# One pool of eight PSUM banks for dense and small products, and the second GLA pair in the order k, q, v, k, q, g

## The chip, the core and the metric

One core of a Trainium2 chip runs the whole program. The metric is the device time of that core in microseconds (us), the median of several executions. TensorE (PE) multiplies, VectorE (DVE), ScalarE (ACT) and GpSimd (POOL) do the element work, and SyncE (SP) issues nearly all DMAs. A PSUM bank takes the output of a matrix product; there are eight of them, each as wide as a 128 x 512 float32 tile.

## The reference, cut to what matters

Two layers on one sequence of 512 tokens, model width 1024. Each layer normalizes x, projects it by one wide matrix `w_in`, and hands the columns to three mixers that work beside each other:

```python
h = rmsnorm(x, norm_mix_g[l])
proj = h @ w_in[l]
y_gla = gla_mixer(a_q, a_k, a_v, a_gk, a_g, ...)      # 4 heads, key 128, value 256
y_ssm = ssd_mixer(b_z, b_xbc, b_dt, ...)              # 4 groups of 8 heads
y_diff = diff_mixer(c_q, c_k, c_v, positions, ...)    # 8 heads, softmax pairs
mixed = (gates[:, :, 0] * (y_gla @ w_br_gla[l]) + gates[:, :, 1] * (y_ssm @ w_br_ssm[l])
         + gates[:, :, 2] * (y_diff @ w_br_diff[l]))
x = x + mixed @ w_out[l]
x = x + jnp.square(jax.nn.relu(rmsnorm(x, norm_mlp_g[l]) @ w_mlp_up[l])) @ w_mlp_down[l]
```

A GLA head needs its own key columns k, query columns q, value columns v and output gate columns g of `proj`; its state runs over chunks of the sequence and its scores carry a decay per key channel. The output is normalized once more at the end.

## The kernel before, in words

All large products are made in float32 precision from three products of rounded parts: a weight block is split into a high part `whi` (ACT) and a rest `wlo` (DVE, or POOL when that ends sooner), the activations lie split in `hl`, and PE adds hi x hi, hi x lo and lo x hi in one bank. Three such products are called a triple below.

The program is written out by a planner that runs in Python before compilation. Class `Flow` keeps a clock of its own (that of PE), a cost model of the engines (`Model`), a list of dense **items** and a list of small **tasks** (generators). `Flow.run` (L445) always serves a task whose wait is met before it takes up a dense step; the order in which PE, ACT, DVE and POOL get their instructions is the order of the planned times. On the chip an engine works through its list in that order and waits on semaphores.

Dense items are of three shapes. `item_a` (L871) makes one 128 x 512 output in one bank, from two half blocks of weights of four triples each; k, q, the SSD inputs and the branch gates are of this shape. `item_a2` (L897) makes two outputs in two banks, for the SSD branch product. `item_w` (L946) makes four 128 x 512 outputs, one per 128 tokens, in four banks that are all open through its eight half blocks of four triples; the value item v and the gate item g of a GLA pair and the q, k, v items (cq, ck, cv) of a differential pair are of this shape. Its first half block asks for the four banks one at a time:

```python
for t in range(NT):
    if i == 0:
        yield {"d": 1}
        it.banks.append(self.T("d"))
```

`refill` (L376) takes the first of the next 28 items whose buffers and conditions are met and loads its weights through SP (L513); two raw weight buffers exist, and four pairs `whi`, `wlo`, of which two are split ahead (`LEAD`).

PSUM is shared out by two tags (L670): `d` with four banks for dense outputs, `m` with four for small products (transposes, scores, states; `psm`, L688). A bank is taken when a product is planned and goes back when its last reader is done. `tag` (L300), `free_at` (L303), `take` (L306) and `next_time` (L338) keep those counts.

A layer's items are listed in `layer` (L1897): `gla_duo` for heads 0 and 1 with the dt item between v and g, four SSD groups (with eight gate items among them, and the branch product of each group after the next group's items), then `gla_duo` (L1340) for heads 2 and 3, the branch product of the last SSD group, two differential pairs, the other 16 gate items, `w_br_gla`, `w_br_diff`, `w_out` and the MLP. For the first pair the items come as v, dt, g and then k, q of both heads; for the second as k, q, k, q, v, g. The items of a pair's v hold four `z4` buffers until both heads have used them, g and each differential item hold two, and there are eight.

`gla_head` (L1394) lists k and q and starts the head's tasks: `gates` (L1415, two DMAs through SP, a small product of the low-rank gate at L1428, logarithms and a scan along the tokens), `keys`, `scores` (L1489: seven levels, each a subtraction on POOL at L1518, two exponentials on ACT, two products with k and q, and small products on PE) and `finish` per chunk. They wait for the events of k and q, and for free `tt` buffers (11 in all).

`step` (L1766) is one softmax step of a differential head; the second differential pair's result goes through `parted` (L1757) to `w_br_diff`, which waits for both pairs.

Of the kernel before, what the change touches and what calls it, by code (L numbers as in the profile page):

```python
# [19 lines left out]
PSUM = bass.MemoryType.PSUM  # L20
# [13 lines left out]
O_Q, O_K, O_V, O_GK, O_G = 0, 512, 1024, 2048, 2064  # L34
# [11 lines left out]
class Event:  # L46
    def __init__(self):
        self.t = None


class Buf:
    def __init__(self, flow, tag, tile_):
        self.flow, self.tag, self.ap, self.rel, self.users = flow, tag, tile_, None, 1
# [12 lines left out]
QN = 6  # L66
FETCH = 4.5
WAKE = 14
LEAD = 2
LAT = {"V": 0.13, "A": 0.1, "G": 0.05}  # L70

# [213 lines left out]
class Flow:  # L285


    def __init__(self, nc):
        self.nc = nc
        self.clock = 0.0  # L290
        self.model = Model(self, nc)
        self.cap, self.pool, self.live = {}, {}, {}
        self.tasks = []
        self.items = []
        self.queue = []
        self.cur = None
        self.hold = None
        self.booked, self.end = [], 0.0

    def tag(self, name, pool, cap):  # L300
        self.cap[name], self.pool[name], self.live[name] = cap, pool, []

    def free_at(self, tag, at):  # L303
        return self.cap[tag] - sum(1 for b in self.live[tag] if b.rel is None or b.rel > at)

    def take(self, tag, shape, dt=F32):  # L306
        live = self.live[tag]
        held = sum(1 for b in live if b.rel is None)
        assert held < self.cap[tag], tag
        b = Buf(self, tag, self.pool[tag].tile(shape, dt, name=tag, bufs=self.cap[tag]))  # L310
        if tag in ("d", "m"):
            self.model.banks.add(b.ap.tensor.name)
        if len(live) >= self.cap[tag]:
            old = min((x for x in live if x.rel is not None), key=lambda x: x.rel)
            self.model.base[b.ap.tensor.name] = old.rel
            live.remove(old)
        live.append(b)
        return b
# [19 lines left out]
    def next_time(self, w):  # L338
        if w is None:
            return self.clock  # L340
        if isinstance(w, (int, float)):
            return w
        if isinstance(w, Event):
            return w.t if w.t is not None else math.inf
        if isinstance(w, dict):
            r = self.clock
            for t, n in w.items():
                rel = sorted(math.inf if b.rel is None else b.rel for b in self.live[t]
                             if b.rel is None or b.rel > self.clock)
                over = len(rel) + n - self.cap[t]  # L350
                if over > 0:
                    r = max(r, rel[over - 1])
            return r
        return max([self.next_time(x) for x in w], default=self.clock)

# [39 lines left out]
    def stage(self):  # L395
# [4 lines left out]
        for j, (_, _, w) in enumerate(self.queue):  # L400
# [4 lines left out]
            if w.bufs is None:  # L405
                if j < LEAD + (self.cur is None) and self.spare("whi"):
                    w.split()
# [246 lines left out]
class Trunk:  # L654
    def __init__(self, tc, ctx, a, out):
        self.tc, self.a, self.out = tc, a, out
        self.ctx = ctx
        self.f = Flow(tc.nc)
        self.halves = [slice(0, S // 2), slice(S // 2, S)]
        self.nc = self.f.model  # L660
        self.const = self.pool("const", 1)
        self.dram = self.pool("dram", 1, space=DRAM)
        self.wp = self.pool("w", 2)
        mx = self.pool("mx", 1)
        self.mx = mx
        self.sm = Ring(self.nc, self.pool("sm", 4), 4)
        self.lp = Ring(self.nc, self.pool("lp", 1), 1)
        pd = self.pool("pd", 1, space=PSUM)
        pm = self.pool("pm", 1, space=PSUM)
        for name, p, cap in (("whi", self.wp, 4), ("wlo", self.wp, 4), ("wraw", self.wp, 2), ("res", mx, KT), ("hl", mx, 10), ("pj", mx, 10), ("z4", mx, 8), ("tw", mx, 3),  # L670
                             ("tt", mx, 11), ("g1", mx, 4), ("d", pd, 4), ("m", pm, 4)):
            self.f.tag(name, p, cap)

    def pool(self, name, bufs, **kw):
        return self.ctx.enter_context(self.tc.tile_pool(name=name, bufs=bufs, **kw))
# [664 lines left out]
    def gla_duo(self, l, duo, h, slot, evy, between=lambda: None, before=()):  # L1340
        nc, a, f = self.nc, self.a, self.f
        w = a["w_in"][l]
        V, G = nc.vector, nc.gpsimd
        first = duo == 0
        shared = {"evv": Event(), "evg": Event(), "r4": (lambda c: h.r4[:, c:c + 1]) if first else None}

        def vg_item(c0, gate):
            key = "g" if gate else "v"

            def fin(it, t, ps):  # L1350
                if first:
                    f.spawn(scaled(it, t, ps))
                else:
                    store(it, t, ps)

            def scaled(it, t, ps):
                yield h.evr4
                store(it, t, ps)

            def store(it, t, ps):  # L1360
                x = it.held[t // 2].ap[:, t % 2]
                if gate:
                    self.act(x, ps.ap, AF.Tanh, scale=h.r4h[:, t:t + 1] if first else 0.5)
                    V.scalar_tensor_tensor(x, x, 1.0, ps.ap, op0=ALU.add, op1=ALU.mult)
                    x2 = x.rearrange("p (h c) -> p h c", c=256)
                    G.tensor_tensor(x2, x2, self.gnr.unsqueeze(1).broadcast_to([P, 2, 256]), op=ALU.mult)
                elif first:
                    r = h.r4[:, t:t + 1]
                    self.act(x, ps.ap, AF.Copy, scale=r)
                    V.scalar_tensor_tensor(it.held[2 + t // 2].ap[:, t % 2], ps.ap, r, x.bitcast(F32),  # L1370
                                           op0=ALU.mult, op1=ALU.subtract)
                else:
                    self.split(x, it.held[2 + t // 2].ap[:, t % 2], ps.ap)
                ps.free()
                if t == NT - 1:
                    for b in it.held:
                        b.users = 2
                    shared[key] = it.held
                    shared["ev" + key].t = f.at(*[b.ap for b in it.held])
            self.item_w(w, c0, h.xg if first else h, fin, extra=[("z4", ([P, 2, S],))] * 2 if gate else  # L1380
                        [("z4", ([P, 2, S], F32R))] * 4, chain=first and not gate)

        def heads():
            for hd in (2 * duo, 2 * duo + 1):
                self.gla_head(l, hd, h, shared, slot, evy[hd], before)
        if not first:
            heads()
        vg_item(O_V + duo * 512, False)
        between()
        vg_item(O_G + duo * 512, True)  # L1390
        if first:
            heads()

    def gla_head(self, l, hd, h, shared, slot, evy, before):  # L1394
        nc, a, f = self.nc, self.a, self.f
# [656 lines left out]
    def load_x(self, ns):  # L2052
# [16 lines left out]
        wake = self.psm()  # L2069
        for i in range(WAKE):  # L2070
            f.tr(wake.ap[:, i % 4 * P:(i % 4 + 1) * P], self.ident, self.ident)
# [137 lines left out]
```

## Time and profile before

| what | value |
|---|---|
| median of 3 runs (lowest to highest) | 2758.38 us (2756.08 to 2759.82) |
| the profiled execution | 2758.74 us |
| its span, first to last instruction | 2756.9 us |
| granted TensorE clock, mean over the span | 0.994 |
| PE busy | 2712.4 us (98%) |
| DVE busy | 1785.3 us (65%) |
| ACT busy | 1311.7 us (48%) |
| POOL busy | 549.0 us (20%) |
| DMA, mean | 107 GB/s |

The page gives the busy time of each engine, the span in 40 slices, and the chain of work that ended last. Other views list who waited for whom, the instructions of a stretch in order of time with the idle time before each in square brackets and what released it, and the busy time of every engine in stretches that one names. A name such as `d<-whi,hl` gives the output tile and the two inputs, the moving operand first: `d<-whi,hl` and `d<-wlo,hl` are the products of an `item_w`, `d<-hl,whi` and `d<-hl,wlo` those of `item_a` and `item_a2`. The planner's helper records most instructions of DVE, ACT and POOL under L83, so tiles and not lines tell them apart. PEclk is the granted share of TensorE's full clock.

### The profile page before, as it was taken

How to read it: one execution, taken by the hardware profiler on the slowest of the kernel's cores; microseconds unless marked ns; L12 is line 12 of the kernel's file. 1: busy time of each engine (PE TensorE's matmuls, PEld its weight loads, DVE VectorE, ACT ScalarE, POOL GpSimd, SP SyncE). 2: the span in 40 equal slices, each digit the busy share in tenths (PEclk: the TensorE clock that was granted, in tenths of full speed). 3: DMA queues.
4: the chain of work that ended last, by engine and by line, in shares of the span. 5: the costliest groups of instructions: out<-in, count | busy, mean ns of one | idle time of the engine just before them, and what ended most of it. 6: DMA issues, size and time to landing. Idle time of an engine off the chain costs nothing.

```text
span 2756.9 us, 40684 instructions
## 1 busy us (share of the span) xinstructions
PE 2712.4 (98%) x14970; PEld 2227.5 (81%) x14970; DVE 1785.3 (65%) x3817; ACT 1311.7 (48%) x2670; POOL 549.0 (20%) x607
## 2 busy tenths in 40 slices
PE   9999999999999999999999999998999999999998
PEld 7788888768888888888877788877788888888887
DVE  7787787766767655444578777677847675644445
ACT  6666555543656333222356664555456652333222
POOL 2313242230221002101012322323222200011001
PEclk9999999999999999999999999999999999999999
DMA  5344434324234433333342443342332344333332
GB/s 163 95 107 128 113 108 134 87 81 126 70 96 122 126 118 97 93 100 97 95 132 74 123 130 103 104 137 76 108 89 84 88 129 146 107 100 98 93 100 85
DMA packets 448644, 293.92 MB, mean 107 GB/s; under 512 B 16614, under 2 KB 409436, under 8 KB 448444
## 3 DMA queue, kind: packets, MB, share of 16 engines
q1 hardware_dynamic: 447828, 290.26, 36.9%
q8 instruction: 118, 1.93, 0.3%
q10 hardware_dynamic: 616, 1.06, 0.1%
q14 instruction: 82, 0.67, 0.1%
HBM read 272.20 MB, written 19.07 MB: 106 GB/s over the span
## 4 chain that ended last, share of the span: by engine, by line
PE 74%; DVE 3%; ACT 1%; DMA 1%; issue 1%; SPq 0%; DVEq 0%; ACTq 0%
PE d L370 66%; PE m L370 6%; PE m L374 2%; DVE rs_t L83 1%; DVE wlo L83 0%; ACT tw L83 0%; DMA wraw<-in_w_in 0%; DVE tt L83 0%; DVE rs_y L83 0%; DVE pj L83 0%; DVE hl L83 0%; ACT whi L83 0%; ACT tt L83 0%; DMA tt<-in_gla_w_gk 0%; DVE g L83 0%
## 5 line engine op out<-in xcount | busy, mean ns | idle before, releaser
L370 PE MATMUL d<-hl,whi 128*128 128x512 f32 (+2 forms) x5696 | 1774.5, 393 | 3.3 <-DVE z L83 1.7
L370 PEld LDWEIGHTS d<-hl,whi 128*128 128x128 f32 (+1 forms) x5696 | 1046.5, 188 | 214.5 <-issue 3.1
L370 PE MATMUL d<-hl,wlo 128*128 128x512 f32 (+2 forms) x2848 | 1108.9, 389 | 6.2 <-DVE wlo L83 6.2
L83 ACT ACTIVATE whi<-wraw 128x512 fp32r<-128x512 f32 x868 | 542.5, 628 | 1044.2 <-PE d L370 956.1
L83 DVE TENSOR_TENSOR wlo<-wraw,whi 128x512 fp32r<-128x512 f32 (+1 forms) x817 | 594.3, 733 | 463.8 <-ACT whi L83 456.2
L370 PEld LDWEIGHTS d<-hl,wlo 128*128 128x128 f32 (+1 forms) x2848 | 533.9, 187 | 122.7 <-DVE wlo L83 9.6
L370 PE MATMUL d<-whi,hl 128*128 128x512 f32 x1280 | 408.7, 401 | 13.4 <-DVE z L83 12.3
L83 POOL TENSOR_TENSOR tt<-tt 128x512 f32<-128x512 f32 x128 | 160.8, 1266 | 942.4 <-ACT hl L83 779.7
L370 PEld LDWEIGHTS d<-whi,hl 128*128 128x128 f32 x1280 | 234.9, 190 | 60.4 <-issue 7.3
L370 PE MATMUL d<-wlo,hl 128*128 128x512 f32 x640 | 252.5, 395 | 3.2 <-DVE wlo L83 3.2
L370 PEld LDWEIGHTS d<-wlo,hl 128*128 128x128 f32 x640 | 121.4, 190 | 30.6 <-DVE wlo L83 4.1
L83 POOL TENSOR_TENSOR wlo<-wraw,whi 128x512 fp32r<-128x512 f32 x51 | 66.5, 1304 | 375.5 <-ACT whi L83 353.6
L83 DVE TENSOR_TENSOR res<-res,d 128x512 f32<-128x512 f32 (+1 forms) x130 | 86.9, 674 | 71.6 <-PE d L370 71.4
L83 DVE SCALAR_TENSOR_TENSOR pj<-d,cols,pj 128x511 f32<-128x511 f32 (+1 forms) x144 | 106.9, 745 | 17.9 <-ACT pj L83 16.0
L83 POOL TENSOR_TENSOR tw<-tw,tt 128x1024 f32<-128x1024 f32 x32 | 79.2, 2474 | 120.1 <-ACT tw L83 120.1
L83 DVE SCALAR_TENSOR_TENSOR tt<-d,tt 128x512 f32<-128x512 f32 x64 | 44.0, 690 | 80.0 <-PE d L370 77.4
L83 ACT ACTIVATE tt<-m 128x512 f32<-128x512 f32 (+5 forms) x132 | 59.0, 452 | 75.1 <-PE m L370 43.4
L83 ACT ACTIVATE tt<-tt 128x256 f32<-128x256 f32 (+3 forms) x190 | 87.6, 499 | 13.5 <-DVE tt L83 10.1
L83 ACT ACTIVATE tw<-tw,acn 128x128 f32<-128x128 f32 x256 | 83.2, 390 | 8.2 <-DMA tw<-acs 8.1
L83 ACT ACTIVATE pj<-m 64x256 fp32r<-64x256 f32 (+1 forms) x160 | 66.2, 420 | 34.9 <-PE m L374 16.4
L370 PEld LDWEIGHTS m<-z,tt 128*128 128x128 f32 x488 | 69.4, 190 | 12.0 <-DVE hl L83 2.5
L370 PE MATMUL m<-z,tt 128*128 128x128 f32 (+1 forms) x488 | 75.4, 284 | 3.4 <-DVE hl L83 2.0
(182 smaller groups left out, 2464.8 us busy)
## 6 DMA issues: line engine op xcount, KB each, us to landing
wraw<-in_w_in SPq DMA_DIRECT2D x224, 512.0 KB
wraw<-in_w_mlp_up SPq DMA_DIRECT2D x64, 512.0 KB
wraw<-in_w_mlp_down SPq DMA_DIRECT2D x64, 512.0 KB
tw<-acs SPq DMA_DIRECT2D x32, 512.0 KB
wraw<-in_w_br_ssm SPq DMA_DIRECT2D x32, 512.0 KB
gates<-tt SPq DMA_DIRECT2D x48, 256.0 KB
tt<-gates SPq DMA_DIRECT2D x48, 256.0 KB
wraw<-in_w_br_gla SPq DMA_DIRECT2D x16, 512.0 KB
```

The costliest lines, as they stand in the source:

```text
L83: fn = lambda a=args, k=kw: real(*a, **k)
L370: self.model.post(self.clock - c, lambda: self.nc.tensor.matmul(out, lhsT, rhs, start=start, stop=stop))
L374: self.model.post(self.clock - 0.109, lambda: self.nc.tensor.transpose(out, in_, ident))
```

## The change

The two tags keep their names, but their tiles now come from one tag `bank` of eight banks in one pool. `d` may hold up to six of them, `m` up to five, both together eight. A tag with a home has two limits, its own and the home's, and every count (free now, free at a time, when next) looks at both. The second pair's items are listed as k, q of head 2, v, k, q of head 3, g, and each head's tasks start with its k and q. The first pair stays as it was. No arithmetic changes, and no item, small product or DMA is added or removed.

```diff
--- before.py
+++ after.py
@@ -66,6 +66,7 @@
 QN = 6
 FETCH = 4.5
 WAKE = 14
+DBANKS, MBANKS = 6, 5
 LEAD = 2
 LAT = {"V": 0.13, "A": 0.1, "G": 0.05}
 
@@ -290,6 +291,7 @@
         self.clock = 0.0
         self.model = Model(self, nc)
         self.cap, self.pool, self.live = {}, {}, {}
+        self.home, self.limits = {}, {}
         self.tasks = []
         self.items = []
         self.queue = []
@@ -297,20 +299,25 @@
         self.hold = None
         self.booked, self.end = [], 0.0
 
-    def tag(self, name, pool, cap):
+    def tag(self, name, pool, cap, home=None):
+
         self.cap[name], self.pool[name], self.live[name] = cap, pool, []
+        self.home[name] = home or name
+        self.limits[name] = [name] + ([home] if home else [])
 
     def free_at(self, tag, at):
-        return self.cap[tag] - sum(1 for b in self.live[tag] if b.rel is None or b.rel > at)
+        return min(self.cap[t] - sum(1 for b in self.live[t] if b.rel is None or b.rel > at)
+                   for t in self.limits[tag])
 
     def take(self, tag, shape, dt=F32):
-        live = self.live[tag]
-        held = sum(1 for b in live if b.rel is None)
-        assert held < self.cap[tag], tag
-        b = Buf(self, tag, self.pool[tag].tile(shape, dt, name=tag, bufs=self.cap[tag]))
-        if tag in ("d", "m"):
+        home = self.home[tag]
+        assert all(self.spare(t) for t in self.limits[tag]), tag
+        b = Buf(self, tag, self.pool[tag].tile(shape, dt, name=home, bufs=self.cap[home]))
+        if home == "bank":
             self.model.banks.add(b.ap.tensor.name)
-        if len(live) >= self.cap[tag]:
+            self.live[tag] = [x for x in self.live[tag] if x.rel is None or x.rel > self.clock] + [b]
+        live = self.live[home]
+        if len(live) >= self.cap[home]:
             old = min((x for x in live if x.rel is not None), key=lambda x: x.rel)
             self.model.base[b.ap.tensor.name] = old.rel
             live.remove(old)
@@ -344,12 +351,13 @@
             return w.t if w.t is not None else math.inf
         if isinstance(w, dict):
             r = self.clock
-            for t, n in w.items():
-                rel = sorted(math.inf if b.rel is None else b.rel for b in self.live[t]
-                             if b.rel is None or b.rel > self.clock)
-                over = len(rel) + n - self.cap[t]
-                if over > 0:
-                    r = max(r, rel[over - 1])
+            for tag, n in w.items():
+                for t in self.limits[tag]:
+                    rel = sorted(math.inf if b.rel is None else b.rel for b in self.live[t]
+                                 if b.rel is None or b.rel > self.clock)
+                    over = len(rel) + n - self.cap[t]
+                    if over > 0:
+                        r = max(r, rel[over - 1])
             return r
         return max([self.next_time(x) for x in w], default=self.clock)
 
@@ -666,10 +674,11 @@
         self.sm = Ring(self.nc, self.pool("sm", 4), 4)
         self.lp = Ring(self.nc, self.pool("lp", 1), 1)
         pd = self.pool("pd", 1, space=PSUM)
-        pm = self.pool("pm", 1, space=PSUM)
         for name, p, cap in (("whi", self.wp, 4), ("wlo", self.wp, 4), ("wraw", self.wp, 2), ("res", mx, KT), ("hl", mx, 10), ("pj", mx, 10), ("z4", mx, 8), ("tw", mx, 3),
-                             ("tt", mx, 11), ("g1", mx, 4), ("d", pd, 4), ("m", pm, 4)):
+                             ("tt", mx, 11), ("g1", mx, 4), ("bank", pd, 8)):
             self.f.tag(name, p, cap)
+        for name, cap in (("d", DBANKS), ("m", MBANKS)):
+            self.f.tag(name, pd, cap, "bank")
 
     def pool(self, name, bufs, **kw):
         return self.ctx.enter_context(self.tc.tile_pool(name=name, bufs=bufs, **kw))
@@ -1380,16 +1389,19 @@
             self.item_w(w, c0, h.xg if first else h, fin, extra=[("z4", ([P, 2, S],))] * 2 if gate else
                         [("z4", ([P, 2, S], F32R))] * 4, chain=first and not gate)
 
-        def heads():
-            for hd in (2 * duo, 2 * duo + 1):
+        def heads(*hds):
+            for hd in hds:
                 self.gla_head(l, hd, h, shared, slot, evy[hd], before)
-        if not first:
-            heads()
-        vg_item(O_V + duo * 512, False)
-        between()
-        vg_item(O_G + duo * 512, True)
         if first:
-            heads()
+            vg_item(O_V, False)
+            between()
+            vg_item(O_G, True)
+            heads(0, 1)
+        else:
+            heads(2)
+            vg_item(O_V + 512, False)
+            heads(3)
+            vg_item(O_G + 512, True)
 
     def gla_head(self, l, hd, h, shared, slot, evy, before):
         nc, a, f = self.nc, self.a, self.f
```

## Rows read from the trace of the kernel before

**Rows 1.** The page: busy time of each engine, share of the span, instructions

```profile
PE 2712.4 (98%) x14970; PEld 2227.5 (81%) x14970; DVE 1785.3 (65%) x3817; ACT 1311.7 (48%) x2670; POOL 549.0 (20%) x607
```

**Rows 2.** Who waited for whom on PE: us in total, times, longest

```profile
PE d L370 <- DVE z L83: 14.0, 7, 7.2
PE d L370 <- DVE wlo L83: 9.4, 7, 3.2
...
PE m L370 <- DVE hl L83: 2.0, 1, 2.0
...
PE m L370 <- DVE g L83: 1.1, 1, 1.1
...
PE m L374 <- DVE g L83: 0.8, 2, 0.6
```

**Rows 3.** Stretches: us, busy (x) of PE, PEld, DVE, ACT, POOL, PEclk, DMA, GB/s

```profile
500.00:600.00 100.00, 91.55 (x644) 71.29 (x643) 68.37 (x124) 49.68 (x98) 32.28 (x34) 0.93 0.26 74
...
1900.00:2000.00 100.00, 91.46 (x758) 73.57 (x757) 81.84 (x218) 48.02 (x113) 25.03 (x19) 0.97 0.31 90
```

**Rows 4.** Order of time on PE, layer 0, second pair: start, us, [idle before]

```profile
535.20 0.74 PE L370 MATMUL d<-whi,hl 128*128 128x512 f32 x2 [0.62 <-DVE z L83]
...
538.54 0.73 PE L370 MATMUL d<-whi,hl 128*128 128x512 f32 x2 [1.37 <-DVE z L83]
...
539.35 0.62 PE L370 MATMUL d<-whi,hl 128*128 128x512 f32 x2
...
540.03 0.61 PE L370 MATMUL d<-whi,hl 128*128 128x512 f32 x2
...
556.65 0.80 PE L370 MATMUL d<-wlo,hl 128*128 128x512 f32 x1 [3.25 <-DVE wlo L83]
...
573.02 1.22 PE L370 MATMUL d<-whi,hl 128*128 128x512 f32 x2 [2.17 <-DVE z L83]
...
576.24 1.22 PE L370 MATMUL d<-whi,hl 128*128 128x512 f32 x2 [0.98 <-DVE z L83]
```

**Rows 5.** The same view, layer 1, from v to g

```profile
1918.07 1.19 PE L370 MATMUL d<-whi,hl 128*128 128x512 f32 x2 [7.18 <-DVE z L83]
...
1919.49 1.05 PE L370 MATMUL d<-whi,hl 128*128 128x512 f32 x2
```

**Rows 6.** Order of time on DVE and on POOL during that wait

```profile
1913.74 1.52 DVE L83 TENSOR_TENSOR wlo<-wraw,whi 128x512 fp32r<-128x512 f32 x1
...
1916.64 0.68 DVE L83 TENSOR_TENSOR wlo<-wraw,whi 128x512 fp32r<-128x512 f32 x1
1917.24 2.47 DVE L83 TENSOR_TENSOR z<-d,z 128x512 fp32r<-128x512 f32 x4
...
1910.65 5.52 POOL L83 TENSOR_TENSOR tt<-tt 128x512 f32<-128x512 f32 x3 [4.35 <-DVE wlo L83]
```

**Rows 7.** Stretches of 10 us in layer 0, columns as in rows 3

```profile
550.00:560.00 10.00, 6.75 (x39) 4.92 (x38) 9.81 (x12) 4.20 (x11) 5.64 (x4) 0.78 0.18 52
...
570.00:580.00 10.00, 6.85 (x53) 4.41 (x54) 8.08 (x13) 2.02 (x6) 6.68 (x6) 0.66 0.20 54
```

**Rows 8.** Order of time on PE: first item_a after g, layer 0, first pair

```profile
63.05 0.73 PE L370 MATMUL d<-hl,whi 128*128 128x512 f32 x2 [1.02 <-DVE z L83]
```

**Rows 9.** PE at layer 0's last differential transpose and w_br_diff

```profile
927.43 0.60 PE L374 MATMUL m<-ident,tt 128*128 128x128 f32 x4
...
938.33 0.50 PE L370 MATMUL d<-hl,wlo 128*128 128x512 f32 x1 [1.66 <-DVE wlo L83]
```

**Rows 10.** Order of time on ACT, layer 0: k and q of head 3, then v

```profile
501.60 0.60 ACT L83 ACTIVATE pj<-d 128x512 f32<-128x512 f32 x1 [1.45 <-PE d L370]
509.20 0.60 ACT L83 ACTIVATE pj<-d 128x512 f32<-128x512 f32 x1 [3.37 <-PE d L370]
532.58 2.64 ACT L83 ACTIVATE z<-d 128x512 fp32r<-128x512 f32 x4 [0.28 <-PE d L370]
```

**Rows 11.** Order of time on PE: gate product of head 3, layer 0

```profile
536.71 0.47 PE L370 MATMUL m<-tt,g 128*128 128x512 f32 x1
```

## The prediction

> **What bounds it now.** I read the page first, then the list of waits of PE, then stretches of 100 us, then the stretches with idle time in order of time. The page says PE: 2712.4 us busy [rows 1] in a span of 2756.9. So only 44.5 us of the span are left to win as idle time, and most stretches have none of it. The list of waits says who ends them [rows 2]: 14.0 us in seven waits for DVE on a tile `z`, 9.4 us in seven for `wlo`, and some single ones of small products. `z` is no input of the product that waits. It is the eviction of the item before: the dense output needs a bank, all four are still held by a v or g item, and DVE has not yet read them.
>
> The two worst stretches hold the second GLA pair of each layer, with 8.45 and 8.54 us idle [rows 3], and both have a granted clock below 1 there. In layer 0 the order of time shows five waits [rows 4]: 0.62 and 1.37 us as g follows v, 3.25 us on a weight rest in the middle of g, 2.17 and 0.98 us as cq follows g. In layer 1 it is one wait of 7.18 us as g follows v [rows 5]. DVE shows why [rows 6]: all four evictions of v run back to back from 1917.24, behind queued work of the last SSD group and weight rests. Some of these took 1.52 us, beside POOL's three subtractions of a head's levels (5.52 us in all), where the same weight rest took 0.68 us once POOL was done. The triple after the wait starts 1.42 us after the first [rows 5], at full rate it is 0.68 us (539.35 to 540.03 in [rows 4]): PE fell idle and came back at the lower of its two clock levels, 1.2 GHz in place of 2.4.
>
> **The change part by part.** Nothing is computed more or less. The sum is made against the profiled execution, 2758.74 us (span 2756.9 and 1.84 around it); the median stands 0.36 lower. About 5.5 us (0.2%) is what a measurement here can tell from nothing.
>
> (A) v to its follower. Before, g wanted four banks at once while v held all four. Now k of head 3 comes after v and wants one, q one more, and up to two of eight are spare if the small products hold two or fewer. Each has eight triples, 8 x 0.68 = 5.4 us, so 10.9 us of work lie between v's end and g, more than the 7.18 us. Gain 0 (small products hold four, no spare) to 7.18 + 0.62 + 1.37 = 9.17 us. I take 9.2: the stretch in question is one where PE had nothing small to do either, so few small banks can be held.
>
> (B) g to cq. The order is as before, four banks after four, but cq's first two find spare ones and the third takes what the first waited for. The bank that came free at 573.02 is then asked for at about 569.9 + 3 x 0.68 = 571.9, so some 1.1 us of the 3.15 stay. I take a gain of 2.0, bounds 0 and 3.15.
>
> (C) The clock behind these waits. In layer 1 two triples at 1.42 in place of 0.68 cost about 1.4 us. In layer 0 a mean of 0.66 over 570 to 580 [rows 7] means 6.8 us at the half level; less the 0.98 us idle inside, 5.8 us of products lost half, 2.9 us. Together 4.3; I take 3.5, bounds 0 and 4.3.
>
> (D) The wait for `wlo` at 556.65, 3.25 us, and its clock: 0.78 over 550 to 560 [rows 7], so from the wait's end to 560 3.35 us at half rate, 1.7 us lost. It comes from DVE, 9.81 us busy of 10. With head 3 listed after v, part of its work leaves this burst; how much no row shows. Bounds 0 and 4.95, I take half, 2.5.
>
> (E) The other `z` waits, 14.0 - 12.3 = 1.7 us, are at a layer's start, where an item of one bank follows a g (one of the two in [rows 8]). One spare bank ends them: 0 to 1.7, I take 1.5.
>
> (F) The small products' own waits for DVE `hl` and `g` are releases of an `m` bank, 2.0 + 1.1 + 0.8 = 3.9 us [rows 2]. A fifth bank ends those where dense items hold at most three. 0 to 3.9, I take 2.0.
>
> (G) What is moved. Head 3's k and q go past v's 32 triples, 21.8 us. On SP their two weight loads go behind v's four, and the two small DMAs of its gates too; on POOL its level subtractions and the clearing of a score tile, on ACT its exponentials move along. That sum is unchanged, and PE covers it where it is busy. That the whole list is planned anew can put waits anywhere. Nearest rows: the 9.4 us of seven `wlo` waits, scattered over both layers. A cost of 0 to 9.4 us; I charge 3, a third, since most of the program has no idle time to lose.
>
> Sum: 9.2 + 2.0 + 3.5 + 2.5 + 1.5 + 2.0 - 3 = 17.7 us, so 2741.0 for the profiled execution and 2741 as a median. With everything gained and no charge, 27.2 us less: 2731.
>
> A rule speaks against the whole list. The `z` waits of rows 2 end with a bank's release, so by the rows a spare bank is worth them. The Trainium skill, "TensorE: Matmul & The Clock Gate", section "HAM oscillation — how this bites in real kernels", reports for a thin matmul that PSUM double-buffering brought no further gain once the loop was reordered. By that, taken as a rule, only D of the gains would count, and with G the sum would be an estimate of 2759.
>
> **Rivals.** (1) The spare bank moves the wait, no more. DVE is what is late in these stretches (9.81 of 10 us [rows 7]), and it also makes the weight rests. If PE runs on into k and q of head 3, it uses up the rests that are split and waits for the next one: A, B and C come back as `wlo` waits, D stays. For it: the 3.25 us wait, and that DVE's late work is not made less. Against it: in layer 1 two rests were done during the wait, at 1915.3 and 1917.3 [rows 6], and two are always split ahead, 5.4 us of PE work, so PE would have been fed. It leaves E, F and G: 2758.7 - 3.5 + 3 = 2758, with half of A 2754. Here the skill's sentence above would be right.
>
> (2) Slower: the differential chain becomes the bound in layer 0. ck needs two `z4` buffers, v holds four until both heads of the pair are done, so a later head 3 delays ck, cv and all softmax steps. Layer 0 has little room: the last transpose of the chain is at 927.43, and `w_br_diff`, with nothing left to put ahead of it, is under way by the wait at 938.33 [rows 9], with a split of the result between them. Price: x us of delay are x us of idle PE there and the clock behind it, 1.4 as in C. The gains of layer 0 (2.0 of A, 2.0 of B, 2.1 of C, 2.5 of D) are lost too, since PE only arrives there sooner; 9.1 of 17.7 stay. The time is 2758.7 - 9.1 + 1.4 + x, slower than can be told from nothing from x = 13 on; x is at most the length of v, 21.8, which gives 2773; I take 2768. Against it: head 3's k and q were ready at 501.60 and 509.20 [rows 10] but its gate product ran only at 536.71 [rows 11], so the chain waits for other things for 27 us, and a shift of 22 mostly fits in there.
>
> (3) The reorder doesn't happen. The planner takes the first item whose buffers are there, and v wants four `z4` at a time when two SSD groups may hold two each. If it finds three, k and q of head 3 pass v as before. Then g follows v with two spare banks: they cover two triples, 1.4 of the 7.18 us, so A loses 5.8, C 1.4 and D all 2.5: 17.7 - 9.7 = 8.0, about 2750. Against it: 8 - 2 - 2 = 4 are free even then.
>
> **How the numbers follow.** The forecast gets 0.60, rival 1 0.17, rival 2 0.13, rival 3 0.10. Faster by over 0.2% are the forecast and most of rival 3 (0.07): 0.67. Within 0.2%: rival 1 and the rest of rival 3, 0.20. Slower: 0.13. The range takes in the full gain, 2730, and goes up over rivals 3 and 1 to the near edge of rival 2, 2765; outside it are most of rival 2 and a replanning that brings more than these terms.
>
> **What would show it.** After, the list of waits should have `z` at 2 us or less in place of 14.0, and no granted clock under 0.9 in a 10 us stretch of the second pair; ACT should show the four evictions of v ahead of head 3's two `pj<-d`. If A is right, PE runs k and q of head 3 right after v with no idle time, and DVE reads v's banks meanwhile. If rival 1 is right, `wlo` waits grow by what `z` lost. If rival 2 is right, PE is idle just ahead of `w_br_diff` of layer 0 for over 10 us. I am wrong in G if idle time turns up in stretches that now have none.

## The result, and the profile after

The changed kernel takes 2738.52 us (median; 2735.54 to 2740.72) beside 2758.14 for the kernel before on the same chip: a ratio of 0.9929, 95% interval 0.9911 to 0.9946. That is 0.7% faster, 2.5 us under the forecast of 2741. The profiled execution took 2735.54 us with a span of 2733.8; it is the shortest of four, of which two (2735.5 and 2736.9 us) have a mean granted clock of 0.997 and two (2740.1 and 2740.7 us) of 0.995. PE's lines have moved by eight (370 is now 378, 374 is 382), line 83 is 84, and both kinds of PSUM tile are called `bank`.

The page's busy line (as [rows 1]):

```profile
PE 2704.3 (99%) x14970; PEld 2225.8 (81%) x14970; DVE 1797.3 (66%) x3824; ACT 1311.2 (48%) x2670; POOL 537.0 (20%) x600
```

The profiled span is 23.1 us shorter. PE's idle time fell from 44.5 to 29.5 us, which is 15.0 of it. Its busy time fell by 8.1 us with the same 14970 matmuls. About half of that, 4.1 us, are products that no longer run at the lower clock; what the other 4.0 are stays open. These are the stretches in which the granted clock was at its lower level while PE had work, four before and two after (columns as in [rows 3]; half of PE's busy time in them is lost, 8.7 and 4.6 us):

```profile
555.61:562.43 6.82, 5.78 (x28) 4.32 (x29) 5.90 (x8) 3.15 (x7) 2.80 (x2) 0.50 0.43 116
572.67:579.50 6.83, 5.50 (x45) 3.60 (x46) 5.41 (x8) 0.00 (x0) 4.89 (x4) 0.50 0.29 79
1548.88:1552.30 3.42, 3.29 (x10) 2.73 (x11) 3.42 (x7) 0.38 (x1) 0.26 (x1) 0.50 0.44 118
1914.11:1920.94 6.83, 2.87 (x7) 2.32 (x8) 6.83 (x11) 2.65 (x8) 2.06 (x2) 0.50 0.28 79
```

```profile
626.59:630.00 3.41, 3.41 (x14) 3.02 (x13) 3.37 (x9) 1.78 (x5) 0.00 (x0) 0.50 0.82 227
2278.64:2285.47 6.83, 5.84 (x13) 4.11 (x14) 3.76 (x7) 1.39 (x3) 0.00 (x0) 0.50 0.46 125
```

Who waited for whom on PE (us in total, times, longest; as [rows 2]):

```profile
PE bank L378 <- DVE wlo L84: 10.4, 6, 3.6
...
PE bank L378 <- DVE z L84: 0.9, 1, 0.9
PE bank L378 <- DVE g L84: 0.9, 1, 0.9
...
PE bank L382 <- DVE g L84: 0.2, 1, 0.2
```

`z` went from 14.0 us to 0.9, and `wlo` from 9.4 only to 10.4. The stretches (columns as in [rows 3]) show where time was won and where some was given back:

```profile
500.00:600.00 100.00, 99.13 (x705) 79.69 (x704) 76.15 (x129) 54.71 (x108) 40.60 (x48) 1.00 0.30 86
600.00:700.00 100.00, 96.41 (x632) 78.95 (x631) 59.37 (x192) 43.19 (x100) 12.48 (x21) 0.98 0.42 119
...
1900.00:2000.00 100.00, 100.00 (x773) 80.71 (x772) 66.51 (x160) 48.35 (x104) 21.88 (x24) 1.00 0.41 123
...
2200.00:2300.00 100.00, 97.06 (x484) 81.14 (x483) 74.75 (x194) 46.96 (x109) 12.95 (x15) 0.97 0.40 124
```

Both second pairs now run at 1.00 (0.93 and 0.97 in [rows 3]) with next to no idle time. The give-backs, in order of time on PE (start, us, in brackets the idle time before):

```profile
201.78 0.50 PE L378 MATMUL bank<-hl,wlo 128*128 128x512 f32 x1 [3.58 <-DVE wlo L84]
...
625.68 0.50 PE L378 MATMUL bank<-hl,wlo 128*128 128x512 f32 x1 [3.05 <-DVE wlo L84]
...
930.27 0.50 PE L378 MATMUL bank<-hl,wlo 128*128 128x512 f32 x1 [1.66 <-DVE wlo L84]
...
2278.53 1.14 PE L378 MATMUL bank<-hl,whi 128*128 128x512 f32 x2 [1.96 <-ACT whi L84]
...
2280.65 0.80 PE L378 MATMUL bank<-hl,wlo 128*128 128x512 f32 x1 [0.98 <-DVE wlo L84]
```

The line at 930.27 answers to [rows 9]: the product `w_br_diff` of layer 0, with the 1.66 us that it waited before. The last two are the same place in layer 1: 2.94 us, where the kernel before had 1.66 too. ACT shows the new order of layer 0: all four evictions of v now begin before those of k and q of head 3 (`pj`), which in [rows 10] came 31 and 23 us ahead of v:

```profile
521.68 1.06 ACT L84 ACTIVATE z<-bank 128x512 fp32r<-128x512 f32 x2
...
529.21 0.58 ACT L84 ACTIVATE z<-bank 128x512 fp32r<-128x512 f32 x1
529.68 0.59 ACT L84 ACTIVATE pj<-bank 128x512 f32<-128x512 f32 x1
...
534.40 0.60 ACT L84 ACTIVATE pj<-bank 128x512 f32<-128x512 f32 x1 [0.33 <-PE bank L378]
```

### The profile page after: what moved, and what is told of

It reads as the page before. It is cut to its first block, busy times and chain, and to the rows that moved or that the text cites. A ratio compares the mean times of both kernels' runs of the same rounds, so it can differ in the third digit from the quotient of the medians.

```text
span 2733.8 us, 40685 instructions
## 1 busy us (share of the span) xinstructions
PE 2704.3 (99%) x14970; PEld 2225.8 (81%) x14970; DVE 1797.3 (66%) x3824; ACT 1311.2 (48%) x2670; POOL 537.0 (20%) x600
## 4 chain that ended last, share of the span: by engine, by line
PE 96%; DVE 3%; ACT 1%; issue 0%; DVEq 0%; POOL 0%; POOLq 0%
PE bank L378 93%; PE bank L382 3%; DVE rs_t L84 1%; DVE rs_y L84 1%; DVE tt L84 0%; DVE wlo L84 0%; DVE pj L84 0%; DVE hl L84 0%; ACT tw L84 0%; DVE g L84 0%; ACT tt L84 0%; ACT whi L84 0%; DVE res L84 0%; ACT pj L84 0%; DVE z L84 0%
## 5 line engine op out<-in xcount | busy, mean ns | idle before, releaser
L378 PE MATMUL bank<-hl,whi 128*128 128x512 f32 (+2 forms) x5696 | 1776.3, 393 | 2.8 <-ACT whi L84 2.0
L378 PEld LDWEIGHTS bank<-hl,whi 128*128 128x128 f32 (+1 forms) x5696 | 1047.7, 188 | 215.3 <-ACT whi L84 3.5
L378 PE MATMUL bank<-hl,wlo 128*128 128x512 f32 (+2 forms) x2848 | 1109.5, 390 | 10.4 <-DVE wlo L84 10.4
L84 DVE TENSOR_TENSOR wlo<-wraw,whi 128x512 fp32r<-128x512 f32 x822 | 604.3, 741 | 457.1 <-ACT whi L84 450.3
L378 PEld LDWEIGHTS bank<-hl,wlo 128*128 128x128 f32 (+1 forms) x2848 | 534.4, 188 | 127.0 <-DVE wlo L84 13.7
L378 PE MATMUL bank<-whi,hl 128*128 128x512 f32 x1280 | 403.9, 397 | 1.8 <-ACT whi L84 1.3
L378 PEld LDWEIGHTS bank<-whi,hl 128*128 128x128 f32 x1280 | 232.9, 188 | 48.3 <-ACT whi L84 1.5
L378 PE MATMUL bank<-wlo,hl 128*128 128x512 f32 x640 | 250.1, 391 | 0.0
L378 PEld LDWEIGHTS bank<-wlo,hl 128*128 128x128 f32 x640 | 120.2, 188 | 26.2 <-DVE wlo L84 0.4
L84 DVE SCALAR_TENSOR_TENSOR pj<-bank,cols,pj 128x511 f32<-128x511 f32 x144 | 107.1, 744 | 12.5 <-ACT pj L84 10.6
```

What stands on the lines that cost most here:

```text
L84: fn = lambda a=args, k=kw: real(*a, **k)
L378: self.model.post(self.clock - c, lambda: self.nc.tensor.matmul(out, lhsT, rhs, start=start, stop=stop))
```

## The experiments

The change has three parts: eight banks shared in place of four and four, limits of six dense and five small tiles, and the new order. The runs take them apart. The kernel before ran beside every group, with medians of 2758.1 to 2759.1, so times of different groups can be set side by side to within one us. The times, but for two runs that fit in no row (the old order in one layer, and the longer hold):

| banks and limits (dense, small) | old order | new order |
|---|---|---|
| two pools, 4 and 4 | 2759 (before) | 2765.0 |
| one pool, 4 and 4 | 2742.9 | 2752.2 |
| one pool, 6 and 5 | 2746.3 | 2738.5 (the change) |
| one pool, 6 and 4; 4 and 5 | | 2752.2; 2749.6 |
| one pool, 5 and 6; 6 and 6; 6 and 8 | | 2738.7; 2735.8; 2755.0 |
| one pool, 4 and 6 | 2798.8 | |

**One half at a time.** The shared pool with six and five and the old order:

```diff
-        def heads(*hds):
-            for hd in hds:
+        def heads():
+            for hd in (2 * duo, 2 * duo + 1):
...
+        if not first:
+            heads()
+        vg_item(O_V + duo * 512, False)
+        between()
+        vg_item(O_G + duo * 512, True)
         if first:
...
-            heads(2)
-            vg_item(O_V + 512, False)
-            heads(3)
-            vg_item(O_G + 512, True)
+            heads()
```

> The shared pool of eight banks (six and five) stays, the second pair's items go back to k, q, k, q, v, g. Theory of the prediction (the spare banks pay, but they need the order): g follows v again and wants four banks, two spare ones cover two triples, 1.4 us of the 7.18; PE's waits for DVE z fall from 14.0 us to about 7, and the time is about 2750 us. Rival, the pool alone pays: 2739 us, z at 1 us. Rival, the order alone pays: 2756 us or more, with z at 12 us or more.

Measured: 2746.27 us, ratio 0.9954 (0.9941 to 0.9966). The time is some 4 us under the expected one, and the reason given for it fell: the waits for `z` are not halved but gone (0.7 us). What layer 1 waits for at its second pair is now `tt`, ahead of small products (PE in order of time):

```profile
1895.34 0.67 PE L378 MATMUL bank<-tt 128*64 128x64 f32 x8 [3.19 <-DVE tt L84]
...
1900.74 0.64 PE L378 MATMUL bank<-tt 128*32 128x32 f32 x16 [4.73 <-ACT tt L84]
```

These 7.9 us stand at the same place as the 7.18 us that the kernel before waited for `z`, so in layer 1 the wait has changed its name here and has not become shorter.

The other half, two pools of four with the new order (the kernel before, with the order of the change):

```diff
-        if not first:
-            heads()
-        vg_item(O_V + duo * 512, False)
...
+            heads(2)
+            vg_item(O_V + 512, False)
+            heads(3)
+            vg_item(O_G + 512, True)
```

> Two pools of four banks as before, only the order of the second pair is the new one. Theory of the prediction: k of head 3 wants one bank while v holds all four, so the wait for v's evictions stays in front of k; only the burst on DVE (term D) gets smaller. z stays at 8 us or more, the time is 2752 to 2756 us. Rival, the order alone pays: 2740 us, z at 2 us.

Measured: 2765.01 us, ratio 1.0021 (1.0011 to 1.0030): slower, and outside what was expected. `z` fell only to 7.9 us, and a new wait shows in both layers, ahead of `w_br_diff`, where the product has to wait for the last of the differential softmax. Who waited for whom on PE, and then PE in order of time:

```profile
PE m L374 <- DVE tt L83: 10.9, 5, 4.6
PE d L370 <- DVE z L83: 7.9, 4, 5.1
```

```profile
935.38 1.12 PE L374 MATMUL m<-ident,tt 128*128 128x128 f32 x4 [4.57 <-DVE tt L83]
938.46 1.22 PE L370 MATMUL d<-hl,whi 128*128 128x512 f32 x2 [1.96 <-ACT whi L83]
...
2305.65 1.12 PE L374 MATMUL m<-ident,tt 128*128 128x128 f32 x4 [4.57 <-DVE tt L83]
2308.72 1.22 PE L370 MATMUL d<-hl,whi 128*128 128x512 f32 x2 [1.96 <-ACT whi L83]
```

This is the place that rival 2 named: head 3's last output comes at 662.17 and 2032.81, in the kernel before at 650.62 and 1997.53. That its buffers are the reason is argued here, and tested in the last run. So the order alone costs 6 us, sharing with higher limits alone gains 13, and both together gain 20.

**Which limit.** The changed kernel with one limit put back to four:

```diff
-DBANKS, MBANKS = 6, 5
+DBANKS, MBANKS = 6, 4
```

> The changed kernel with at most four small products' banks in place of five, six for dense products. Theory of the prediction: the dense products' spare banks pay, the fifth small bank only term F, 2 us: 2739 to 2743 us, z at 1 us. Rival, the fifth small bank pays: 2750 us or more.

```diff
-DBANKS, MBANKS = 6, 5
+DBANKS, MBANKS = 4, 5
```

> The changed kernel with at most four banks for dense products in place of six, five for small ones. Theory of the prediction: no spare bank for k of head 3, so the z waits come back, 8 us or more of them, and the time is 2750 to 2755 us. Rival, the fifth small bank pays: 2740 us.

Measured: 2752.20 us (0.9974, 0.9964 to 0.9983) and 2749.64 us (0.9965, 0.9953 to 0.9978). Neither has a wait for `z`, the second with a dense limit of four as before: the limit isn't what ends those waits. Both show the wait at rival 2's place. These are the lines of six and four in order of time:

```profile
938.04 1.12 PE L382 MATMUL bank<-ident,tt 128*128 128x128 f32 x4 [3.84 <-DVE tt L84]
941.12 1.22 PE L378 MATMUL bank<-hl,whi 128*128 128x512 f32 x2 [1.96 <-ACT whi L84]
...
2292.63 1.12 PE L382 MATMUL bank<-ident,tt 128*128 128x128 f32 x4 [4.77 <-DVE tt L84]
2295.71 1.22 PE L378 MATMUL bank<-hl,whi 128*128 128x512 f32 x2 [1.96 <-ACT whi L84]
```

**Sharing by itself.** One pool of eight with the limits of before, with the old order (the lines of the first run besides) and with the new one:

```diff
-DBANKS, MBANKS = 6, 5
+DBANKS, MBANKS = 4, 4
```

> The shared pool of eight banks, but with limits of four dense and four small tiles, so the same limits as before, and the old order k, q, k, q, v, g. Only which bank a tile is handed differs from before. Theory now (the waits for z came from a tile being given the very bank that was just planned free; in a pool of eight the next tile gets one that has been free for longer): PE's waits for z are under 2 us (14.0 before), and the time is 2746 to 2752 us against 2759. Rival (the limits six and five are what takes the waits away): z waits stay at 9 to 14 us and the time is 2756 to 2761.

> Limits of four and four in the shared pool, with the new order. Theory: no z waits (under 2 us, where two pools of four with the new order had 7.9), but head 3 of the first GLA layer ends later than about 655 us and the differential chain becomes the bound ahead of the multiplication by the last branch's output, with over 4 us of PE waits there in each layer: 2750 to 2756 us. Rival (sharing alone is enough and the limits don't matter): 2736 to 2742, with under 2 us of waits there.

Measured: 2742.94 us with the old order (0.9943, 0.9930 to 0.9957) and 2752.23 with the new one (0.9976, 0.9967 to 0.9986). The plan counts the same tiles under the same limits, and its result is the same too: the first of these kernels issues the instructions of the kernel before, all of them in the same order on every engine, and the second those of the two pools with the new order. Only the bank that a tile is given differs. That alone is worth 15.8 us with the old order and 12.8 with the new one.

How it works can be seen at v of layer 1. The kernel before, ACT's and DVE's evictions of v's four banks:

```profile
1908.45 1.06 ACT L83 ACTIVATE z<-d 128x512 fp32r<-128x512 f32 x2
...
1910.83 1.06 ACT L83 ACTIVATE z<-d 128x512 fp32r<-128x512 f32 x2
```

with DVE's four following from 1917.24 and PE idle for 7.18 us up to 1918.07 [rows 5, 6]. One pool, four and four, old order, the same instructions on ACT, DVE and PE in order of time:

```profile
1896.96 1.06 ACT L84 ACTIVATE z<-bank 128x512 fp32r<-128x512 f32 x2
...
1899.31 1.06 ACT L84 ACTIVATE z<-bank 128x512 fp32r<-128x512 f32 x2
...
1905.76 2.47 DVE L84 TENSOR_TENSOR z<-bank,z 128x512 fp32r<-128x512 f32 x4
...
1899.30 0.73 PE L378 MATMUL bank<-whi,hl 128*128 128x512 f32 x2
...
1900.79 0.61 PE L378 MATMUL bank<-whi,hl 128*128 128x512 f32 x2
...
1904.00 0.78 PE L378 MATMUL bank<-whi,hl 128*128 128x512 f32 x2 [2.37 <-ACT tt L84]
```

DVE is just as late: its four come 6.45 us after ACT's second pair (6.41 before). But g's first triples run at 1899.30, 6.5 us before DVE begins to read v's banks, so they were not written into one of them. Among four, g's first tile gets the bank that the plan has just counted as free, and any lateness of DVE against the plan is a stall. Among eight that are handed round between dense and small tiles, it gets one that was free long before. What is left is 2.37 us until ACT has read `tt` from the bank of a small product. The trace doesn't name banks, but the programs that the two kernels build do, and their products on PE come in the order of the traces. In the kernel before, v of layer 1 lies in banks 2, 1, 3 and 0, and g gets these four again. With one pool v lies in 2, 3, 0 and 4, and g gets 1, 6, 7 and 5; bank 5 held the small product that ACT had still to read. In nearly all cases a tile gets the free bank whose last reader stands furthest back in the program.

**More small banks.** Six small tiles with six dense ones:

```diff
-DBANKS, MBANKS = 6, 5
+DBANKS, MBANKS = 6, 6
```

> The changed kernel with six small banks allowed in place of five. Theory (small banks let head 3 end early, which is what the last branch waits for in layer 1): PE idle ahead of that branch in layer 1 falls from 2.9 us to 1.7 and the time is 2732 to 2737. Rival (the sixth small bank only takes a bank from the dense stream, or the planner's order merely shuffles): 2737 to 2745, with new waits for the evictions z or pj.

Measured: 2735.77 us, ratio 0.9919 (0.9906 to 0.9933), which can't be told from the changed kernel's 0.9929 (0.9911 to 0.9946). The wait ahead of layer 1's last branch fell to 1.66 us as the theory said, and waits for weight rests grew elsewhere (PE in order of time):

```profile
581.17 0.80 PE L378 MATMUL bank<-wlo,hl 128*128 128x512 f32 x1 [5.66 <-DVE wlo L84]
...
2282.82 0.50 PE L378 MATMUL bank<-hl,wlo 128*128 128x512 f32 x1 [1.66 <-DVE wlo L84]
```

Six dense and eight small tiles, and five and six:

```diff
-DBANKS, MBANKS = 6, 5
+DBANKS, MBANKS = 6, 8
...
-DBANKS, MBANKS = 6, 5
+DBANKS, MBANKS = 5, 6
```

> The changed kernel with no limit on small tiles other than the eight banks (eight in place of five). Theory: the softmax chain is no longer than with six (187 us or less), waits ahead of the last branch's product are 1.7 us at most in both layers, and what is left is 8 to 15 us of waits for weight splits (wlo) wherever VectorE falls behind: 2731 to 2740. Rival (with no limit small work takes the banks and the dense stream waits for its own evictions): waits for z, g or pj of over 6 us and 2742 to 2755.

> The changed kernel with limits of five dense and six small tiles. If what counts is the sharing and the small limit of six, it is as fast as with six and six (2733 to 2739). If the sixth dense bank matters, head 3 ends later (past 660 us in layer 0) and waits of over 3 us stand ahead of the last branch's product: 2742 to 2750.

Measured: 2755.0 us (0.9985, 0.9976 to 0.9994) and 2738.71 us (0.9929, 0.9917 to 0.9941). Five and six does as well as the changed kernel. With six and eight the time is that of the rival but not its reason: waits for `g` and `pj` are 1.5 and 3.3 us, and idle time and slow clock sit around 190 to 260 and 570 to 660 instead, a scatter of waits of up to 4.8 us on PE, such as

```profile
636.66 0.79 PE L378 MATMUL bank<-hl,wlo 128*128 128x512 f32 x1 [4.76 <-DVE wlo L84]
```

**Old order in one layer.** Limits of six and five, the new order in layer 0 alone:

```diff
+        elif l:
+            heads(2, 3)
+            vg_item(O_V + 512, False)
+            between()
+            vg_item(O_G + 512, True)
         else:
             heads(2)
```

> Limits of six and five, the new order in layer 0 and the old one in layer 1. Theory (each layer's waits belong to its order): layer 1 shows the two waits for small products near its second pair of 3 to 5 us each that the old order had, and no stall over 1.7 us ahead of the last branch's product: 2739 to 2744. Rival (the old order's waits in layer 1 came from what layer 0 left behind): those waits are absent and the time is 2730 to 2736, below both kernels.

Measured: 2748.10 us, ratio 0.9962 (0.9950 to 0.9975). Layer 1 has the waits of the old order with these limits again (3.20 and 4.75 us, at 1894.70 and 1900.10) and 1.66 us ahead of its last branch, as the theory said. The time is 4 us above its band, which the theory doesn't explain, and 2 above the old order in both layers, where the two intervals overlap.

The old order in both layers, as in the first run, with

```diff
-DBANKS, MBANKS = 6, 5
+DBANKS, MBANKS = 4, 6
```

> The shared pool with the old order, limits of four dense and six small tiles (against four and four in the run that gave 2742.9 us). Theory: the length of the softmax chain, from its first tw to its last, follows the limit on small tiles (202 us with four, 196 to 202 with five, 186 with six), so both chains take 184 to 190 us here; the old order ends head 3 early in any case, so no wait over 1.7 us stands ahead of the last branch's product either way, and the time moves little: 2738 to 2745. Rival (the small limit speeds up the GLA heads themselves, not only the softmax chain): the waits for small products near the second pair of layer 1 go too, and the time is 2728 to 2737, below the changed kernel.

Measured: 2798.80 us, ratio 1.0146 (1.0132 to 1.0160): far from both. In layer 0 nothing is new. In layer 1 the plan put sixteen gate tiles ahead of head 3's last products (ACT evicts them from 1983.71 to 2079.61), and PE waited 1.3 us for the weights of every second one. Head 3's last output came at 2100.62, some 70 to 120 us later than in the other kernels, and the k product of the differential branch at 2119.27. The softmax then ended behind the dense stream, and eight waits of over 0.8 us stand on PE between 2299 and 2342 (19.0 us in all), among them

```profile
2338.88 1.11 PE L382 MATMUL bank<-ident,tt 128*128 128x128 f32 x4 [5.19 <-DVE tt L84]
```

at a granted clock of 0.67 from 2300 to 2345. So the latest start of that chain goes with the slowest kernel. These waits are not all of it: PE is idle for 73.0 us here and for 29.5 in the changed kernel. The theory that the chain's length follows the small limit fell as well: from its first `tw` to its last it takes 187 us with six and six, 191 with six and eight and 186 in layer 1 here, but 199 in layer 0 here and 201 in layer 0 with five and six, about what the kernels with four or five small tiles have (196 to 204). What sets it stays open.

**The hold, made longer.** The last run tests rival 2 by its cause. In the changed kernel v's and the gate's `z4` buffers are let go 20 us later in the plan when head 3 is done:

```diff
+        def drop(bufs):
+            def late(at):
+                yield at
+                for x in bufs:
+                    x.free()
+            f.spawn(late(f.clock + (20.0 if hd == 3 else 0.0)))
...
-                for x in shared["g"]:
-                    x.free()
+                drop(shared["g"])
```

and the same for v's. PE's order is that of the changed kernel up to there.

> The changed kernel, with the z buffers of the second GLA pair (v's and the gate's) let go 20 us later in the plan, in both layers; nothing else differs, and the order is that of the changed kernel up to there. Theory (the differential attention's k product waits for these buffers, and its softmax chain, about 200 us long, is what the last branch's product waits for): the evictions of that product start some 20 us later (about 694 us in layer 0, 2059 in layer 1), the 64 lines of dense matmuls that come forward in the order fill the time there, and the waits ahead of the last branch's product grow to 5 to 12 us in each layer (1.7 and 2.9 in the changed kernel); with the clock that falls behind them 2747 to 2760 us. Rival (the chain has slack, or its length shrinks by as much): no new wait there and 2735 to 2742.

Measured: 2761.97 us, ratio 1.0011 (1.0002 to 1.0020), so 23.4 us above the changed kernel and 2 above the band. The k product's evictions on ACT in order of time, at 673.73 and 2038.51 in the changed kernel:

```profile
697.04 1.28 ACT L84 ACTIVATE z<-bank 128x512 f32<-128x512 f32 x2 [0.28 <-PE bank L378]
...
2070.79 1.28 ACT L84 ACTIVATE z<-bank 128x512 f32<-128x512 f32 x2 [0.27 <-PE bank L378]
```

and PE ahead of the last branch:

```profile
935.84 1.09 PE L382 MATMUL bank<-ident,tt 128*128 128x128 f32 x4 [5.10 <-DVE tt L84]
938.89 1.22 PE L378 MATMUL bank<-hl,whi 128*128 128x512 f32 x2 [1.96 <-ACT whi L84]
...
2301.90 1.09 PE L382 MATMUL bank<-ident,tt 128*128 128x128 f32 x4 [5.28 <-DVE tt L84]
2304.94 1.22 PE L378 MATMUL bank<-hl,whi 128*128 128x512 f32 x2 [1.96 <-ACT whi L84]
```

From head 3's last output to these evictions it is 52.7 and 53.4 us, against 30.9 and 31.6 in the changed kernel: the hold moves the chain by 21.8 in both layers. The waits grow from 1.66 to 7.06 us in layer 0 and, with those from 2284 on, from 2.94 to 12.57 in layer 1: 15.0 us together. PE's busy time grows by 10.5 (2704.3 to 2714.8), and with the 15.0 that is the 25.5 us by which the profiled spans differ. The lower clock makes up 9.3 of the 10.5: 6.1 behind the new waits (0.77 over 930 to 940, 0.50 over 2290 to 2310) and 3.2 behind two waits that the changed kernel has too (see the last section). The waits grew where the theory put them, so the buffers' hold is a cause; the 3.2 us are not its doing as far as the traces show.

## Why the prediction was right, and where it was not

The number was right: 17.7 us forecast, 23.2 gained in the profiled execution, 19.6 between the medians. Steps C and E held; A and F had about the right size for a reason that the runs don't bear out; D and G were sized too small, and their errors cancel in part.

**A and B**, the waits for `z` in the second pairs: all 12.3 us are gone, where I took 11.2 (9.2 and 2.0; of B's 3.15 I had left 1.1). The size is right, the reason of A is not. I argued that g has to be put off, so that k and q of head 3 lie between, and that with the old order two spare banks would cover two triples and leave 5.8 of 7.18 us. At layer 1's place, the old order with four and four leaves no wait for `z` and 2.37 us for `tt`; with the two spare banks of six and five 0.7 us for `z` stand behind 7.9 for `tt`. The step that failed is the count of spare banks. The wait was not for a number of banks but for one particular bank, and the spare ones were there all the time, in the other pool.

**C and D**: the clock is 1.00 in both second pairs, and the wait of 3.25 us for a weight rest at 556.65 is gone. I took half of D. C's two low stretches cost 4.2 us (4.3 reckoned). D's cost 2.9 and not 1.7, since the lower level lasted to 562.43 and I had read it up to 560 alone. That moving head 3 is what ends D fits the runs at four and four: the wait is there with the old order (3.88 us at 553.91) and not with the new one. With six and five it is gone under the old order too.

**E** went as said, and **F**, taken at 2.0, measured 2.8: of 3.9 us for `hl` and `g` 1.1 are left. The fifth bank for small products isn't the reason: with six and four none of these waits is left either.

**G** was sized too small. Idle time other than that of A, B, D, E and F was 23.4 us before (44.5 less 21.1) and is 28.4 now: 5.0 us, where I charged 3 in all. The lower clock at two new places costs 4.6 us on top, against 1.6 at 1548.88 that went. The sign that I had named is there. Idle time turned up where PE had been at 100.00, for one in this stretch, before and after:

```profile
700.00:800.00 100.00, 100.00 (x535) 84.71 (x534) 75.40 (x225) 61.01 (x155) 24.97 (x36) 1.00 0.30 81
```

```profile
700.00:800.00 100.00, 98.26 (x520) 82.75 (x519) 74.15 (x212) 57.95 (x142) 25.20 (x41) 1.00 0.27 77
```

**The rule against the list.** By the sentence of the Trainium skill that I cited ("TensorE: Matmul & The Clock Gate", "HAM oscillation — how this bites in real kernels"), the banks would have brought nothing and the time been about 2759. Here, with all instructions the same, other banks brought 15.8 us. The sentence is about another kernel's loop; the row of 14.0 us for `z` was the better guide.

**Rival 1** is out: `wlo` waits grew by 1.0 us as `z` lost 13.1. **Rival 3** is out by ACT's lines above. **Rival 2** didn't decide, but it is the most real of the three. With the new order at four and four, the waits at `w_br_diff` are 9.7 us (two pools) and 9.9 us (one pool) longer in both layers together than with the old one, and the times 6 and 9 us. I had named the right buffers and the right place, and erred in three things. I looked at layer 0 alone, and the changed kernel is short of room in layer 1. I wrote that layer 0 has little room, but 21.8 us of delay brought 5.4 us of new waits there. And I put its fate on head 3's spare 27 us, while the limits shift it: with the new order head 3 of layer 0 ends at 660.0 at four and four and at 642.8 at six and five, in the kernel before at 650.6. That isn't all of it: with six and six and with five and six it ends at 657.3 and 657.8, and no wait over 1.66 us follows at `w_br_diff` in that layer.

So the change works by three effects whose size hangs on what is already there: sharing −15.8, the order +9.3 on top of it, and the higher limits −13.7 on top of both, with which the waits at `w_br_diff` that the order brings are mostly gone. With the old order the same limits cost 3.3. That the whole plan shifts with every limit is part of these figures; only the first is free of it. None of the versions beats the changed kernel by more than can be measured.

## What to carry to other kernels

When a wait ends with the release of a buffer, ask which buffer the next tile was given and whether another was free; a planner with times of its own should hand out the one longest free, since that absorbs what the chip is late. Try the allocation alone, with every instruction in its place, before moving work. And before an item is put later, look for the buffers that it keeps from a long chain elsewhere: the bill came nearly 300 us on.

## What the runs showed that I had not expected

The length of a wait didn't tell whether the clock falls. In the changed kernel the wait of 3.58 us at 201.78 left the granted clock at 1.00, and the shorter one of 3.05 us at 625.68 did not (10-us stretches, columns as in [rows 7]):

```profile
200.00:210.00 10.00, 8.22 (x45) 6.99 (x46) 9.27 (x18) 4.11 (x8) 1.59 (x4) 1.00 0.53 134
...
620.00:630.00 10.00, 6.95 (x62) 5.60 (x61) 9.71 (x40) 4.64 (x11) 1.31 (x1) 0.83 0.35 105
```

The kernel with the longer hold, whose order on PE is the same up to there, has the first of these waits at the same length, and in its profile the lower clock followed:

```profile
201.98 0.79 PE L378 MATMUL bank<-hl,wlo 128*128 128x512 f32 x1 [3.58 <-DVE wlo L84]
```

```profile
200.00:210.00 10.00, 8.02 (x38) 6.78 (x39) 7.96 (x16) 3.73 (x7) 0.79 (x1) 0.83 0.51 133
```

So the same wait cost 1.5 us of slower products in one profiled execution and nothing in the other. A wait of 1.48 us behaves likewise, though the order has changed by then: at 760.48 in the changed kernel the clock stays (1.00 over 760 to 770), at 783.79 with the longer hold it falls (0.83 over 780 to 790, 1.7 us lost). These two are the 3.2 us above. Behind its new waits, 15.0 us in all, the longer hold lost 6.1 us, about the share that C had (4.3 behind 12.3).
